# A hybrid RWKV/convolution trunk: a smaller descriptor memory, five raw weight buffers instead of three, three split pairs instead of two

## The chip, the cores and the metric

The kernel runs on one core of one Trainium2 chip. The metric is device time in microseconds of one execution. Before the change the median of three runs is 1274.27 us (1272.84 to 1274.8).

## The reference

One layer over 1024 tokens of width 1024, all in float32. A token mixer has an RWKV-7 recurrence on half of its channels (8 heads of 64) and a gated causal convolution of width 31 on the other half; both take their inputs from one projection and meet in one output projection. A gated feed-forward part with a causal convolution of width 3 follows. Each part stands between two RMS norms and has a residual connection.

```python
h = _rms_norm(x, norm_pre_mix[i])
mix, v_first = _hybrid_mixer(h, w_in_i, ...)     # p = h @ w_in; _wkv7; conv; ... @ w_out
x = x + _rms_norm(mix, norm_post_mix[i])
h = _rms_norm(x, norm_pre_ffn[i])
hid = _causal_dwconv(h @ ffn_up, ffn_conv_w, ffn_conv_b)      # 1024 -> 2 * 2816
gate, up = hid[..., :D_FF], hid[..., D_FF:]
x = x + _rms_norm((jax.nn.gelu(gate) * up) @ ffn_down, norm_post_ffn[i])
```

## The kernel before, in words

Every large product is made at float32 accuracy from three products of a faster kind. An operand is split in a high and a low part: ScalarE (ACT) casts the float32 tile to the rounded type, which gives the high part, and another engine subtracts that from the original, which gives the low part (`split`, L159 to L162). The matmuls are high times high, high times low and low times high; low times low is left out.

**Weights** come through `weight` (L164 to L184). It allocates a raw tile from the pool `wp` under the tag `wr`, which has three buffers, has SyncE (SP) issue the load (L170), allocates a pair `wh` and `wl` with two buffers each (L176), and splits: ACT makes `wh`, GpSimd (POOL) makes `wl`. In the last part, `ffn_down`, VectorE (DVE) makes `wl`. All of this is traced under a raised priority. A raw, `wh` or `wl` tile is 128 partitions by 512 float32, 2 KB of a partition. One pair feeds 12 matmuls of 512 columns. Some weights bypass the pair: those that `ffn_down` holds elsewhere (`held`), and those of the second half of the output projection (`home`). Weights of the input projection are used for both halves of the sequence; the first half stores the low part in HBM, and the second half loads it back (L178, L179, L183).

Three more places take a buffer of `wr` or of the pair: the two small LoRA matrices at the start (L236), and in `shared` the tile `t3` (L1023) and the pairs of the combined weights (L1028).

**The order of the work.** The sequence is worked on in two halves of 512 tokens, the recurrence in four quarters of 256 with four chunks of 64 each. `mixer` (L1245) writes down streams with priorities: the recurrence comes ahead of the norms, the convolution and the projections, so that the matmuls of the projections fill what the recurrence leaves free on TensorE. `w_out` (L794 on) multiplies a half by the output projection and stores it in `mixd`. `norm_ffn` (L839) loads `x` and `mixd` rows, makes the first norm of the FFN and its transposed, split activations `f`. The first 12 feed-forward column pairs of the first half (`ffn_pair`, L901) run beside the last quarter of the recurrence. `gates`, `ffn_pair` for the second half and `shared` (L1004) follow: the last ten column pairs, and the down projection, use a two-by-two scheme with seven block products instead of eight, for which weights and activations are added and subtracted. POOL makes these sums of weights (`four_sums` and `weight_sums`, L1054 to L1081).

Each engine runs its own instructions strictly in order, and SP issues nearly all DMAs in order. Where an instruction stands in its engine's order is not written by hand: `build` opens

```python
with tile.TileContext(nc, schedule_with_timeline_sim=True) as tc, ExitStack() as ctx:
```

which orders the traced instructions by priority along a simulated time line. The number of buffers enters this simulation, since an instruction that allocates a tile is held there until a buffer of its tag is free.

`kernel` (L1462) creates the program. A part of each SBUF partition is reserved for descriptors of DMAs that software generates, 16 KB unless said otherwise.

Of the kernel before, what the change touches and what calls it, by code (L numbers as in the profile page):

```python
# [13 lines left out]
F32 = mybir.dt.float32  # L14
F32R = mybir.dt.float32r
# [7 lines left out]
P = 128  # L23
# [3 lines left out]
HALF = 512  # L27
# [4 lines left out]
D_RWKV = 512  # L32
# [10 lines left out]
LN_EPS = 1e-5  # L43
GN_EPS = 64e-5

HELD = 5
DECAY = math.exp(-0.5)

# [50 lines left out]
class Trunk:  # L99
# [64 lines left out]
    def weight(self, src, shape, home=None, held=None, kept=None):  # L164


        with self.tc.high_priority():
            raw = (self.f2p.tile(shape, F32, tag="f2", name=self.nm("wr")) if held is self.hp else
                   self.wp.tile(shape, F32, tag="wr", bufs=3, name=self.nm("wr")))
            self.load = self.nc.sync.dma_start(raw, src)  # L170
            if held:
                hi, lo = self.pair("w", held)
            elif home:
                hi, lo = (home[0].tile(shape, F32R, tag=t, bufs=BUFS[t], name=self.nm("wm")) for t in home[1:])
            else:
                hi, lo = (self.wp.tile(shape, F32R, tag=t, bufs=2, name=self.nm(t)) for t in ("wh", "wl"))  # L176
            if kept and kept[0]:
                self.nc.scalar.copy(hi, raw)  # L178
                self.nc.sync.dma_start(lo.bitcast(F32), kept[1])  # L179
            else:  # L180
                self.low = self.split(hi, lo, raw, self.low_pool)[1]
        if kept and not kept[0]:
            self.nc.sync.dma_start(kept[1], lo.bitcast(F32))  # L183
        return hi, lo  # L184
# [31 lines left out]
    def setup_mixer(self, ctx):  # L216
        nc, tc, a = self.nc, self.tc, self.a
        pool = lambda name, bufs=1: ctx.enter_context(tc.tile_pool(name=name, bufs=bufs))
        cp = pool("mconst")
        self.mix = pool("mix")  # L220
        self.banks = {"pb": 2, "pc": 1, "pe": 2}
        self.xs = [self.psum.tile([P, 512], F32, name=f"xs{g}") for g in range(2)]
        self.wa = cp.tile([P, HALF], F32, name="wa")

        self.dw = cp.tile([P, 16 + 1024], F32, name="dw")
        nc.gpsimd.memset(self.dw[0:64, 528:1040], 0.0)
        self.Y = self.psum.tile([P, 512], F32, name="Y")


        self.lora = cp.tile([G_LORA, D_RWKV], F32, name="lora")
        nc.sync.dma_start(self.lora, a["lora"][:G_LORA, 2])
        self.lw = cp.tile([96, 2, D_RWKV], F32R, name="lw")
        for e in range(2):
            raw = self.wp.tile([P, D_RWKV], F32, tag="wr", bufs=3, name=self.nm("wr"))  # L236
            nc.sync.dma_start(raw, a["lora"][:, e])
            nc.scalar.copy(self.lw[:, e], raw[0:96])
            low = self.lw[64:96, e]
            nc.gpsimd.tensor_tensor(low, raw[64:96], low.bitcast(F32), ALU.subtract)  # L240
        self.lx = cp.tile([96, 2, QUARTER], F32R, name="lx")
        n = POFF["k_k"]
        self.omu = cp.tile([P, n], F32, name="omu")
        nc.vector.tensor_scalar(self.omu, self.params[:, :n], -1.0, 1.0, ALU.mult, ALU.add)

        self.hw0 = cp.tile([P, 8], F32, name="hw0")
        nc.vector.tensor_scalar(self.hw0, self.params[:, POFF["w0"]:POFF["w0"] + 8], 0.5, None, ALU.mult)
        self.ka = cp.tile([P, 8], F32, name="ka")
        ka = self.params[:, POFF["k_a"]:POFF["k_a"] + 4]
        nc.vector.tensor_scalar(self.ka[:, 0:4], ka, 0.5, None, ALU.mult)  # L250
        nc.vector.tensor_scalar(self.ka[:, 4:8], ka, -0.5, 1.0, ALU.mult, ALU.add)
        cw = self.params[:, POFF["cw"]:POFF["cw"] + 4 * CONV_W]
        nc.vector.tensor_scalar(cw, cw, 0.5, None, ALU.mult)
        self.carry = cp.tile([P, n], F32, name="carry")
        self.ccarry = cp.tile([P, 4, 32], F32, name="ccarry")[:, :, :CONV_W - 1]
# [748 lines left out]
    def shared(self, i, S, A22, act0, act1, raws):  # L1004

        nc = self.nc
        temp = lambda: self.f2p.tile([P, HALF], F32, tag="f2", name=self.nm("acc"))
        kview = lambda t: t.rearrange("p (k m) -> p k m", k=4)
        up = self.a["ffn_up"]

        def add(out, x, y):
            with self.tc.high_priority():
                nc.vector.tensor_tensor(out, x, y, ALU.add)

        if raws is None:
            T = lambda n: self.weight(kview(self.usums[n - 1]), [P, 4, P])
            b22 = lambda: self.weight(up[FT + i, 1], [P, 4, P])
        else:
            with self.tc.high_priority():
                b11, b12, b21, b22r = raws  # L1020
                for n in (1, 3, 0, 2):
                    self.load = nc.sync.dma_start(kview(raws[n]), up[n % 2 * FT + i, n // 2])
                t3 = self.wp.tile([P, HALF], F32, tag="wr", bufs=3, name=self.nm("t3"))  # L1023
                self.four_sums(b11, b12, b21, b22r, t3)

            def pair(raw):
                with self.tc.high_priority():
                    hi, lo = (self.wp.tile([P, HALF], F32R, tag=t, bufs=2, name=self.nm(t)) for t in ("wh", "wl"))  # L1028
                    self.low = self.split(hi, lo, raw, True)[1]
                return kview(hi), kview(lo)  # L1030

            T = lambda n: pair((b12, b11, t3, b21)[n - 1])
            b22 = lambda: pair(b22r)
        x, y, z = (self.bank() for _ in range(3))
        self.four(x, T(2), S[2], True, True)
        add(act1, act1, x)
        self.four(y, T(1), S[1], True, True)
        W = temp()
        add(W, act1, y)
        self.four(z, T(3), S[3], True, True)  # L1040
        add(x, W, z)
        self.four(y, b22(), S[4], False, True)
        add(y, act1, y)
        self.four(z, T(4), A22, False, True)
        add(z, act1, z)
        two = [temp() for _ in range(2)]
        self.taps(0, i, 1, y, two[0])
        nc.vector.tensor_tensor(act0, act0, two[0], ALU.mult)
        self.taps(1, i, 0, z, act1)
        nc.scalar.activation(z, act1, AF.Gelu_apprx_tanh)  # L1050
        self.taps(1, i, 1, x, two[1])
        nc.vector.tensor_tensor(act1, z, two[1], ALU.mult)
# [50 lines left out]
    def ffn_down(self, acts):  # L1103
# [58 lines left out]
        def hold(j, every=2):  # L1162

            if j % every == 1 and len(late) < HELD:
                late.append(self.weight(B(1, 1)(HT - HELD + len(late)), [P, 512], held=self.hp))

# [294 lines left out]

# [6 lines left out]
```

## Time and profile before

| what | value |
|---|---|
| median of 3 runs | 1274.27 us |
| the profiled execution | 1273.13 us |
| its span, first to last instruction | 1271.4 us |
| mean granted TensorE clock | 0.990 |
| raw weight loads, L170 | 256 KB each, 2.7 to 2.9 us from issue to landing |
| cast to `wh`, 128x512 | 0.62 us on ACT |
| `wl` on POOL, 128x512 | 1.31 us mean |
| `wl` on DVE, 128x512 | 0.69 us |
| DMA traffic | 185.70 MB, 146 GB/s on average |

PE is TensorE's matmuls and PEld its weight loads, which run beside them. Matmul ends are modelled, so a matmul of 512 columns is drawn with 0.39 us. In the view of waits a row says which engine and output tile waited, for what, the total in us, how many times, and the longest. L135 is the line of every matmul, L150 of every transpose, and L162 of every split, so the tile names tell which one is meant: `wh` and `wl` are weights, `h` and `f` activations, `pb`, `pe`, `xs`, `Y` and `pc` PSUM banks, `a` and `w` the split operands that `ffn_down` keeps elsewhere. SPq stands for a DMA issue on SP. A wait for several things is put down to the one that came last.

### The profile page before, as it was taken

Reading aid. Unit: us, or ns where it says so; the run is one execution under the profiler, and the core shown is the slowest. Engines: PE = TensorE matmul, PEld = TensorE weight load, DVE = VectorE, ACT = ScalarE, POOL = GpSimd, SP = SyncE. Lnnn points to the kernel's source line nnn. Section 1 sums busy time; section 2 is a strip of 40 time slices with the busy share of each in tenths; the row PEclk is TensorE's granted clock in tenths of the full one; section 3 lists DMA queues with packets and bytes.
Section 4 is the critical chain, followed back from the end, with each engine's and each line's share of the span. In section 5 each row is a group of like instructions: output and inputs, shape, how many; then the busy total and the mean of one; then the engine's idle time right before and its main releaser. Section 6 shows DMA issues by size and latency. Waiting matters only on the chain.

```text
span 1271.4 us, 23025 instructions
## 1 busy us (share of the span) xinstructions
PE 1220.3 (96%) x8460; PEld 990.1 (78%) x8460; DVE 891.2 (70%) x1540; ACT 731.1 (58%) x1518; POOL 495.4 (39%) x438
## 2 busy tenths in 40 slices
PE   6999989999999988999999999999999999999996
PEld 4767767787778877788789878778877888888885
DVE  5286998998679989997631165666356779479667
ACT  7563563655845766566744277776555556545451
POOL 4343320011113332344455369898588860000001
PEclk9999998999999999999999999999999999999999
DMA  7644342343343451232345398888522236336523
GB/s 242 173 133 141 117 134 75 94 134 124 110 135 86 122 183 66 85 84 84 101 132 166 112 336 299 292 305 268 173 65 73 79 127 222 99 98 194 173 76 133
DMA packets 105505, 185.70 MB, mean 146 GB/s; under 512 B 15184, under 2 KB 21712, under 8 KB 105392
## 3 DMA queue, kind: packets, MB, share of 16 engines
q1 hardware_dynamic: 105392, 184.23, 46.2%
q8 instruction: 67, 1.10, 0.4%
q14 instruction: 46, 0.38, 0.1%
HBM read 141.58 MB, written 42.60 MB: 145 GB/s over the span
## 4 chain that ended last, share of the span: by engine, by line
PE 55%; DVE 8%; DMA 3%; POOL 3%; issue 2%; ACT 2%; SPq 0%; POOLq 0%; DVEq 0%; ACTq 0%
PE pb L135 26%; PE pe L135 13%; PE xs L135 11%; PE Y L135 2%; DVE pc L416 2%; PE pc L135 2%; POOL wl L162 1%; DVE nrow L1116 1%; DVE x L1100 1%; POOL b L1056 1%; PE pc L150 1%; DMA pt<-mixd 1%; DMA m<-mixd 1%; PE pe L150 0%; DMA b<-ffn_down 0%
## 5 line engine op out<-in xcount | busy, mean ns | idle before, releaser
L162 POOL TENSOR_TENSOR wl<-wr,wh 128x512 fp32r<-128x512 f32 (+1 forms) x181 | 237.2, 1312 | 247.7 <-ACT wh L162 221.0
L162 ACT CAST wh<-wr 128x512 fp32r<-128x512 f32 (+1 forms) x220 | 135.5, 616 | 170.7 <-issue 43.9
L135 PE MATMUL pb<-h,wh 128*128 128x512 f32 (+3 forms) x720 | 229.5, 398 | 2.5 <-ACT wh L162 1.0
L135 PE MATMUL pb<-f,wh 128*128 128x512 f32 x696 | 219.0, 395 | 2.6 <-ACT wh L162 1.5
L416 DVE SCALAR_TENSOR_TENSOR pc<-c,params,pc 128x512 f32<-128x512 f32 x232 | 174.1, 750 | 8.8 <-ACT pc L413 4.8
L135 PEld LDWEIGHTS pb<-h,wh 128*128 128x128 f32 (+2 forms) x720 | 131.8, 188 | 34.9 <-ACT wh L162 2.6
L135 PEld LDWEIGHTS pb<-f,wh 128*128 128x128 f32 x696 | 130.0, 189 | 31.0 <-ACT wh L162 2.8
L135 PE MATMUL pb<-h,wl 128*128 128x512 f32 (+3 forms) x360 | 146.4, 407 | 2.3 <-POOL wl L162 2.1
L135 PE MATMUL pb<-f,wl 128*128 128x512 f32 x348 | 137.9, 397 | 1.5 <-POOL wl L162 1.5
L157 POOL TENSOR_TENSOR ss<-var,mhalf 128x1 f32<-128x1 f32 x16 | 11.0, 692 | 222.6 <-DVE ss L1097 198.2
L1056 POOL TENSOR_TENSOR b<-b,b 128x512 f32<-128x512 f32 x66 | 86.8, 1317 | 2.8 <-issue 0.9
L135 PE MATMUL pe<-f,wh 128*128 128x512 f32 x272 | 84.2, 391 | 0.1
L135 PEld LDWEIGHTS pb<-h,wl 128*128 128x128 f32 (+2 forms) x360 | 67.7, 188 | 20.7 <-POOL wl L162 4.5
L135 PEld LDWEIGHTS pb<-f,wl 128*128 128x128 f32 x348 | 65.7, 189 | 16.9 <-POOL wl L162 3.1
L135 PE MATMUL xs<-f,wh 128*128 128x512 f32 x200 | 62.0, 391 | 0.4 <-DVE act L953 0.4
L135 PEld LDWEIGHTS pe<-f,wh 128*128 128x128 f32 x272 | 50.9, 188 | 10.6 <-ACT wh L162 0.3
L899 DVE SCALAR_TENSOR_TENSOR pt<-pb,params,pt 128x511 f32<-128x511 f32 (+1 forms) x48 | 35.7, 743 | 30.0 <-ACT ecarry L892 29.5
L162 POOL TENSOR_TENSOR wl<-b,wh 128x512 fp32r<-128x512 f32 x36 | 47.0, 1307 | 21.7 <-ACT wh L162 19.8
L135 PE MATMUL pe<-f,wl 128*128 128x512 f32 x136 | 53.7, 395 | 0.7 <-POOL wl L162 0.7
L706 POOL TENSOR_TENSOR XG<-r,GE 64x256 f32<-64x256 f32 x30 | 20.4, 683 | 86.9 <-DVE r L725 82.0
L178 ACT CAST wh<-wr 128x512 fp32r<-128x512 f32 (+2 forms) x44 | 26.5, 604 | 43.1 <-PE pb L135 31.2
L162 ACT CAST wh<-b 128x512 fp32r<-128x512 f32 x36 | 22.2, 617 | 46.8 <-PE pb L135 18.9
(428 smaller groups left out, 2883.7 us busy)
## 6 DMA issues: line engine op xcount, KB each, us to landing
wr<-ffn_up SPq DMA_DIRECT2D x117, 256.0 KB, 2.8
wr<-w_in SPq DMA_DIRECT2D x80, 256.0 KB, 2.9
b<-ffn_down SPq DMA_DIRECT2D x44, 256.0 KB, 4.4
sums<-b SPq DMA_DIRECT2D x44, 256.0 KB, 4.0
wr<-sums SPq DMA_DIRECT2D x44, 256.0 KB, 2.7
lows<-wl SPq DMA_DIRECT2D x40, 256.0 KB, 3.3
wl<-lows SPq DMA_DIRECT2D x40, 256.0 KB, 2.7
b<-ffn_up SPq DMA_DIRECT2D x40, 256.0 KB, 2.7
```

The costliest lines, as they stand in the source:

```text
L135: return self.nc.tensor.matmul(out, lhsT, rhs, start=start, stop=stop, skip_group_check=skip)
L150: self.nc.tensor.transpose(out, in_, self.con("ident")[:n, :n])
L157: self.nc.gpsimd.tensor_tensor(out, v[:, :n], self.mhalf[:, :n], ALU.pow)
L162: return self.nc.scalar.copy(hi, src), eng.tensor_tensor(lo, src, hi.bitcast(F32), ALU.subtract)
L178: self.nc.scalar.copy(hi, raw)
L416: nc.vector.scalar_tensor_tensor(out, c[:, j:j + HALF], w(j), acc, ALU.mult, ALU.add)
L706: nc.gpsimd.tensor_tensor(x[64:128], R[64:128, gs], w.GE[64:128, c, gs].unsqueeze(2).broadcast_to([64, 4, CH]), ALU.mult)
L899: nc.vector.scalar_tensor_tensor(acc[:, o:], ps[:, :HALF - o], w(j), acc[:, o:], ALU.mult, ALU.add)
L1056: sub = lambda o, x, y, op=ALU.subtract: self.nc.gpsimd.tensor_tensor(o, x, y, op)
L1100: nc.vector.scalar_tensor_tensor(x, f[c], s[:, 1:2], x, ALU.mult, ALU.add)
L1116: nc.vector.tensor_tensor(out, a, b, op)
```

## The change

The raw tag gets five buffers instead of three, `wh` and `wl` get three each instead of two, at all places that name them, and the descriptor memory is set to 1024 bytes of a partition.

```diff
+RAW = 5
+PAIRS = 3
...
-                   self.wp.tile(shape, F32, tag="wr", bufs=3, name=self.nm("wr")))
+                   self.wp.tile(shape, F32, tag="wr", bufs=RAW, name=self.nm("wr")))
...
-                hi, lo = (self.wp.tile(shape, F32R, tag=t, bufs=2, name=self.nm(t)) for t in ("wh", "wl"))
+                hi, lo = (self.wp.tile(shape, F32R, tag=t, bufs=PAIRS, name=self.nm(t)) for t in ("wh", "wl"))
...
-            raw = self.wp.tile([P, D_RWKV], F32, tag="wr", bufs=3, name=self.nm("wr"))
+            raw = self.wp.tile([P, D_RWKV], F32, tag="wr", bufs=RAW, name=self.nm("wr"))
...
-                t3 = self.wp.tile([P, HALF], F32, tag="wr", bufs=3, name=self.nm("t3"))
+                t3 = self.wp.tile([P, HALF], F32, tag="wr", bufs=RAW, name=self.nm("t3"))
...
-                    hi, lo = (self.wp.tile([P, HALF], F32R, tag=t, bufs=2, name=self.nm(t)) for t in ("wh", "wl"))
+                    hi, lo = (self.wp.tile([P, HALF], F32R, tag=t, bufs=PAIRS, name=self.nm(t)) for t in ("wh", "wl"))
...
-    nc = bacc.Bacc("TRN2", target_bir_lowering=False, num_devices=1)
+    nc = bacc.Bacc("TRN2", target_bir_lowering=False, num_devices=1, dynamic_dma_scratch_size=1024)
```

## The prediction

> **What bounds the kernel now.** I read the span on the page first, then busy time by stage, then the waits of TensorE (PE, and PEld for its weight loads), and last the time lines around single waits. The stages, from the view by windows, say which engine sets the time:
>
> ```profile
> span 1271.4 us, 23025 instructions
> ```
> ```profile
> 32.00:456.00 424.00, 409.47 (x3808) 326.38 (x3808) 340.26 (x609) 250.39 (x502) 105.19 (x112) 0.98 0.41 121
> 456.00:497.00 41.00, 34.76 (x420) 26.31 (x416) 35.45 (x85) 28.28 (x74) 10.60 (x14) 0.96 0.43 147
> 497.00:1245.00 748.00, 739.74 (x4072) 607.89 (x4072) 476.86 (x744) 427.17 (x885) 360.09 (x283) 1.00 0.49 155
> ```
>
> A row of the second fence is one stretch: its length, then busy time of PE, PEld, DVE, ACT and POOL, the granted clock, the DMA share and GB/s. PE is the bound. It is idle 14.5 us in the mixer (32 to 456), 6.2 us in the handover to the FFN (456 to 497) and 8.3 us in the 748 us of FFN. No count of matmuls changes, so the change can win only idle time and stretched matmuls. Which of it belongs to weights, the waits of PE and PEld say; columns are total us, times, longest. First PE and PEld in the stretch 0 to 500, then both from 500 to 1050:
>
> ```profile
> PE pb L135 <- POOL wl L162: 3.0, 5, 1.1
> ...
> PE pb L135 <- ACT wh L162: 1.0, 1, 1.0
> PE pb L135 <- ACT wh L178: 0.9, 1, 0.9
> ```
> ```profile
> PEld pb L135 <- POOL wl L162: 5.5, 7, 1.5
> ...
> PEld pb L135 <- ACT wh L162: 2.9, 5, 1.2
> ```
> ```profile
> PE pb L135 <- ACT wh L162: 2.0, 3, 1.2
> PE pb L135 <- POOL wl L162: 1.9, 3, 0.9
> PE pe L135 <- ACT wh L162: 0.8, 1, 0.8
> PE pe L135 <- POOL wl L162: 0.7, 1, 0.7
> PE xs L135 <- POOL wl L162: 0.7, 2, 0.3
> ```
> ```profile
> PEld pe L135 <- POOL wl L162: 4.2, 11, 1.1
> PEld xs L135 <- POOL wl L162: 4.1, 9, 0.8
> PEld pb L135 <- POOL wl L162: 3.9, 6, 1.3
> PEld pb L135 <- ACT wh L162: 3.8, 4, 1.6
> ```
>
> So PE stands still for a split weight for 4.9 us in 7 waits before 500, and for 6.1 us in 10 waits after it: the largest removable item of the FFN's 8.3 us. PEld waits for the same tiles 8.4 us before and 16.0 us after. The true loss lies between, since a weight load that is late by less than its lead costs nothing.
>
> **Why a weight is late.** One wait in full, from the time line (start, length, what, idle time before it in brackets):
>
> ```profile
> 625.38 0.62 ACT L162 CAST wh<-wr 128x512 fp32r<-128x512 f32 x1
> ...
> 630.77 0.63 ACT L162 CAST wh<-wr 128x512 fp32r<-128x512 f32 x1
> ...
> 631.46 0.73 PE L135 MATMUL pb<-f,wh 128*128 128x512 f32 x2 [1.19 <-ACT wh L162]
> ```
> ```profile
> 1075.21 1.36 PE pe L135 x6
> ```
>
> ACT makes two casts of weights 5.4 us apart, because other work of ACT stands between them. The row in the second fence is PE at its pace, from the chain that ended last: 6 matmuls in 1.36 us, 0.227 us each. A weight pair feeds 12 matmuls, so 2.72 us. Two pairs last 5.4 us, one of them already in use: a burst of that length on ACT or POOL empties them. Three last 8.2 us.
>
> **The change part by part.** Descriptor memory: who uses DMA descriptors in memory is told by the queues.
>
> ```profile
> q1 hardware_dynamic: 105392, 184.23, 46.2%
> q8 instruction: 67, 1.10, 0.4%
> q14 instruction: 46, 0.38, 0.1%
> ```
>
> All of the program's data goes through one hardware queue, issued by SP, and the rest is instruction fetch; no queue of descriptors made by software exists. Cost of the smaller memory: 0, with nothing needed to hide it. It adds and removes no instruction. It frees 15 KB of a partition, and the tiles (2 KB each) take two raws and one pair, 8 KB.
>
> Third pair: the longest wait of PE is 1.2 us and of PEld 1.6 us, both below the 2.72 us that one more pair holds, so each single wait is covered if the engines get the time to fill the third pair beforehand. After 500 the loss is 6.1 us plus what the row of a matmul hides: the profile draws a matmul longer than its pace, 0.73 us for two against 0.45, so up to 0.28 us of each wait counts as busy. With 0.15 us each for 10 waits that is 7.6 us; PEld's 16.0 is the upper bound and 6.1 the lower. I take 9, nearer the PE rows, because most PEld waits have no PE wait behind them. I credit three quarters of it, 6.75 us, not all: in the worst part the filler itself is nearly full, as this row shows (POOL is the fifth engine).
>
> ```profile
> 768.00:800.00 32.00, 32.00 (x148) 26.30 (x147) 17.87 (x29) 23.94 (x52) 30.81 (x25) 1.00 0.87 297
> ```
>
> Before 500 the loss is 4.9 to 8.4 us, 6 to 7 by the same reckoning, and I credit 2.8: PE's time there is handed on only where PE decides. The first w_out matmuls wait for the recurrence, not for weights, and the handover is a chain of transfers, of which these are the first two:
>
> ```profile
> PE pe L150 <- DVE mixr L760: 2.2, 1, 2.2
> ```
> ```profile
> 456.50 4.28 DMA mixd<-t
> 461.22 3.37 DMA row<-x
> ```
>
> Five raws: they let SP issue loads earlier. What it waits for, and what ACT waits for:
>
> ```profile
> SPq L170 <- POOL wl L162: 52.7, 10, 18.3
> ```
> ```profile
> ACT wh L162 <- PE pb L135: 62.8, 39, 2.5
> ```
>
> The first is SP's wait for a raw buffer between 425 and 520, 5.3 us each on average; the second is ACT's wait to overwrite a pair that PE still reads, over the whole span. Both block work queued behind on the same engine. I book no gain of their own for them: a raw that comes earlier helps only through the pair it fills. No bytes are added, so the DMA share is unchanged in sum.
>
> What is added: nothing executes twice, but build() orders all engines by a simulated time line, so every order can move. No row prices that. The handover's idle time, 6.2 us, is the nearest row: it could double or go, so plus or minus 6.2, and I take 0 because it has no direction.
>
> One cost has one. When POOL splits a weight while DVE reads two operands from SBUF, DVE stretches:
>
> ```profile
> 70.50 0.68 DVE L493 TENSOR_TENSOR l<-row,pt 128x512 f32<-128x512 f32 x1
> ...
> 72.45 3.29 POOL L162 TENSOR_TENSOR wl<-wr,wh 128x512 fp32r<-128x512 f32 x2
> ...
> 74.64 1.66 DVE L510 TENSOR_TENSOR l<-pt,pt 128x512 f32<-128x512 f32 x1
> ```
>
> 0.98 us longer for the same shape. A pair that is filled ahead lets POOL run splits back to back, as in these two. I charge one such collision, 1.0 us, at places where DVE is on the path. [...]
>
> **The sum.** 6.75 + 2.8 - 1.0 = 8.5 us gained. The profiled execution took 1273.13 us, 1.7 over its span and 1.1 under the median of 1274.27; taken off the profiled execution that is 1264.6, on the scale of the median 1265.8, my forecast.
>
> **Rivals.** (a) More: ACT's 62.8 us of waiting go as well, and the evacuations queued behind come earlier. Half of the mixer's 14.5 us of idle PE would go on top, 7.2: 1258.6. For it: 39 such waits. Against it: in the mixer ACT is busy only 250 of 424 us, so what is queued behind those waits has room to catch up. (b) Rate, not depth: the filling engine is late in a row rather than in a burst, or the planner leaves the new buffers empty. POOL's 30.81 of 32 us speaks for it, PE's 17 waits, spread over both stretches with none above 1.2 us, against it. A quarter of 8.5 is left, 2.1: 1272.2, no change. [...] (d) Slower: the handover. Weight loads have high priority and SP issues in order. With more raws, further ffn_up loads can stand in SP's queue ahead of the row and mixd loads of the first FFN norm, each waiting for POOL to free a raw. Two such waits at 5.3 us lengthen the chain of transfers that begins above by 10.5; with only the gain of the FFN, 6.75, left, the result is 3.8 slower, 1278.1. It decides from the second wait on, and PE has no other work there. Against it: a larger supply also lets SP finish those loads before the handover begins.
>
> **How the numbers follow.** Forecast 0.50, (a) 0.12, (b) 0.17, (c) 0.05, (d) 0.16. About 0.2%, 2.5 us, is what a measurement of this kernel can tell from no change. Faster is the forecast with (a), 0.62; same is (b) with (c), 0.22; slower is (d), 0.16. The likeliest case's own range is 1260 to 1271, the gain between 3 and 14. The range is 1256 to 1278: it takes in (a), (b), (c) and most of (d), and the re-ordering's 6.2 us around the forecast; a cure of all 24 us of PEld waits lies outside, as does (d) with a third blocked load.
>
> **What would show it.** If right: PE's waits for wh and wl fall from 11.0 us to about 3 and PEld's from 24 to below 12; what is left lies between 730 and 1050; PE's busy time falls by the stretched matmuls, 2 to 4 us; ACT's waits on pb before wh shrink; SP's wait for a raw shrinks; the FFN stretch from the end of the handover to the last products is 5 to 8 us shorter. [...] The forecast is wrong if the wh and wl waits go and the span does not follow, or if the gain sits in the handover instead.

## The result: 10 us slower, the loss in the mixer

The changed kernel takes 1284.62 us, the median of four runs from 1282.96 to 1289.17, beside 1274.20 (1272.84 to 1274.80) for the kernel before: a ratio of 1.0089, with an interval of 1.0062 to 1.0116. The forecast was 1265.8 in a range of 1256 to 1278.

The profiled execution of the changed kernel is its longest, 1289.17 us at a mean granted clock of 0.968; the other three took 1282.96 to 1284.71 us at 0.976 to 0.978. So the two traces differ by 15.8 us of span where the medians differ by 10.4, and some 5 us of what the trace shows belong to this execution alone. Its code lies two lines lower, so L137, L152 and L164 are the matmuls, transposes and splits. From the page, the span and the granted clock in 40 slices:

```profile
span 1287.2 us, 23033 instructions
...
PEclk8999977999998988999999999999999999999998
```

The view by windows of the changed kernel, over the three stretches of the prediction (length, then busy us and instructions of PE, PEld, DVE, ACT and POOL, granted clock, DMA share, GB/s):

```profile
32.00:456.00 424.00, 403.22 (x3495) 318.43 (x3494) 317.61 (x579) 237.26 (x461) 97.70 (x105) 0.94 0.39 113
456.00:497.00 41.00, 34.69 (x452) 29.21 (x450) 32.10 (x54) 26.01 (x71) 13.23 (x12) 0.90 0.51 161
497.00:1245.00 748.00, 741.95 (x4281) 618.20 (x4282) 479.86 (x778) 435.18 (x906) 362.43 (x292) 0.99 0.49 158
```

Read the count behind PE first: in the 424 us of the mixer it has done 3495 matmuls, where it did 3808 before. The stretches no longer hold the same work, so their busy times cannot be subtracted. A fair cut is an event of the program: the first matmul of the FFN (`pb<-f,wh`) starts at 497.65 us before and at 528.16 after. Cut there, the same view, first of the kernel before:

```profile
32.00:497.00 465.00, 444.22 (x4222) 352.69 (x4220) 375.72 (x693) 278.67 (x576) 115.78 (x126) 0.98 0.41 124
497.00:1262.00 765.00, 756.52 (x4145) 621.44 (x4144) 492.02 (x779) 429.35 (x891) 365.28 (x289) 1.00 0.49 155
```

and of the changed kernel:

```profile
32.00:528.00 496.00, 464.70 (x4222) 369.57 (x4220) 377.69 (x704) 283.67 (x580) 115.98 (x126) 0.93 0.39 116
528.00:1278.00 750.00, 748.16 (x4144) 623.38 (x4144) 482.23 (x769) 427.94 (x889) 363.00 (x288) 1.00 0.49 157
```

Now the counts agree, and the change does two opposite things. The same 4222 matmuls up to the FFN take 496 us in place of 465; the same 4144 after it take 750 in place of 765. To a tenth, from the first FFN matmul to the last of the down projection, it is 750.0 in place of 764.1. The FFN won 14.1 us and the mixer lost 30.5.

The FFN's win is the one that was aimed at. Waits of PEld for a split weight over the whole span of the changed kernel (total us, times, longest):

```profile
PEld pb L137 <- ACT wh L164: 1.3, 1, 1.3
PEld xs L137 <- ACT wh L164: 0.8, 1, 0.8
PEld pe L137 <- ACT wh L180: 0.4, 1, 0.4
PEld pe L137 <- ACT wh L164: 0.4, 1, 0.4
PEld xs L137 <- POOL wl L164: 0.3, 1, 0.3
```

Single waits are left, and in the waits of PE itself, where 17 had stood, neither `wh` nor `wl` occurs any more. The largest waits of PE that are left, apart from the 9.5 us at the start (9.9 before):

```profile
PE xs L152 <- DVE r L727: 4.1, 3, 3.0
PE pe L152 <- ACT ck L558: 3.7, 2, 3.0
PE pb L152 <- DVE h L281: 3.0, 4, 1.4
PE pe L152 <- DVE mixr L748: 2.7, 2, 2.1
PE xs L137 <- ACT l L653: 2.6, 2, 1.9
```

The third is a wait for activations and stood at 2.5 us before. The other four are for results of the recurrence, and nothing filled PE while it waited for them.

**Where the loss begins.** The recurrence's first chunk, seen by its operations with each shape apart (count: duration in ns min/median/max, first and last start in us). The kernel before:

```profile
L135 PE MATMUL pe<-dw,l x128: 177/178/198, 134.5 to 136.5; 32*32 32x16 f32 x128
L150 PE MATMUL pe<-const,l x32: 187/188/202, 151.0 to 155.0; 32*32 32x32 f32 x32
...
L704 ACT COPY XG<-xs x32: 344/368/371, 166.2 to 596.8; 64x256 f32<-64x256 f32 x32
```

The changed kernel:

```profile
L137 PE MATMUL pe<-dw,l x128: 177/178/198, 142.6 to 144.6; 32*32 32x16 f32 x128
L152 PE MATMUL pe<-const,l x32: 188/188/199, 166.8 to 172.6; 32*32 32x32 f32 x32
...
L706 ACT COPY XG<-xs x32: 347/368/371, 178.9 to 636.3; 64x256 f32<-64x256 f32 x32
```

None of these operations is longer; each starts later. The small matmuls of the recurrence are 8.1 us late at the first row, the transposes 15.8, the first chunk's `XG` 12.7, and the last chunk's `XG` 39.5. What stands ahead of the transposes, the chain of waits of the changed kernel says, asked for 60 to 206 us (start, length, what):

```profile
146.72 1.62 PE pe L137 x2
148.34 5.26 PE pb L137 x18
153.60 2.01 PE pe L137 x129
155.61 5.45 PE pb L137 x24
161.06 0.24 PE pe L137 x2
161.30 5.22 PE pb L137 x23
```

The `pb` rows are projections. The row of 129 holds a second group of small matmuls of the recurrence, `pe<-l,dw`, which follows the one listed above; it starts at 141.80 us before and 153.53 after. The matmuls that read `h`, from the first group to the second and from the second to the transposes (PE busy and count, clock, DMA share, GB/s), before:

```profile
134.51:141.80 7.29, 4.67 (x19) 1.00 0.45 146
141.80:150.99 9.19, 7.22 (x31) 1.00 0.47 125
```

and after:

```profile
142.56:153.53 10.97, 6.25 (x19) 0.84 0.34 97
153.53:166.80 13.27, 11.35 (x49) 1.00 0.56 159
```

So the lateness has three parts here. The first group is 8.1 us late: the steps of DVE ahead of it are 4.5 us late at the first (`dw<-l`, 115.9 to 120.4), shortly after the chain has come over from PE's projections, and 7.0 at the last (`l<-dw`, 129.9 to 136.9). Up to the second group the delay grows to 11.7 us with the same 19 projection matmuls: PE waits 2.0 us for DVE's `kk`, and the granted clock is 0.84. Up to the transposes it grows to 15.8, because 49 projection matmuls stand ahead of them in PE's order where 31 had stood.

Projections are the work that is meant to fill gaps. How much of it PE does in two longer stretches, the same view tells, before:

```profile
96.00:134.00 38.00, 30.67 (x119) 1.00 0.44 130
176.00:204.00 28.00, 10.31 (x38) 0.88 0.24 76
```

and after:

```profile
96.00:134.00 38.00, 32.94 (x132) 1.00 0.51 149
176.00:204.00 28.00, 1.65 (x3) 0.53 0.06 20
```

Thirteen more are done in the first stretch (29 more counted from 32 us, 376 in place of 347), and then, while the recurrence's small serial steps run and the second half's activations are not ready, 3 are left in place of 38. The granted clock there is 0.53. The skipped time is not made up: the last projection matmul ends at 403.7 us in place of 385.8, and `w_out` of the first half begins at 413.1 in place of 389.9. The delay of 12.7 us at the first chunk is thus 23.2 at `w_out` and 30.5 at the first FFN matmul; which wait adds which part on the way was not followed.

### The profile page after: what moved, and what is told of

Its sections match the earlier page's. It is cut to its first block, busy times and chain, and to the rows that moved or that the text cites. A ratio compares the mean times of both kernels' runs of the same rounds, so it can differ in the third digit from the quotient of the medians.

```text
span 1287.2 us, 23033 instructions
## 1 busy us (share of the span) xinstructions
PE 1231.5 (96%) x8460; PEld 1008.4 (78%) x8460; DVE 884.4 (69%) x1540; ACT 734.9 (57%) x1520; POOL 494.1 (38%) x438
## 4 chain that ended last, share of the span: by engine, by line
PE 83%; DVE 10%; ACT 3%; DMA 2%; issue 1%; SPq 0%; POOL 0%; DVEq 0%; POOLq 0%; ACTq 0%
PE pb L137 42%; PE pe L137 18%; PE xs L137 17%; PE Y L137 2%; DVE pc L418 2%; PE pc L137 2%; PE pe L152 1%; PE pc L152 1%; DVE sub L593 1%; DMA mixd<-t 0%; DVE h L281 0%; PE xs L152 0%; DMA l<-x 0%; DVE dw L595 0%; DVE dw L584 0%
## 5 line engine op out<-in xcount | busy, mean ns | idle before, releaser
L164 POOL TENSOR_TENSOR wl<-wr,wh 128x512 fp32r<-128x512 f32 (+1 forms) x181 | 235.7, 1305 | 233.7 <-ACT wh L164 211.7
L137 PE MATMUL pb<-h,wh 128*128 128x512 f32 (+3 forms) x720 | 232.8, 400 | 2.4 <-DVE row L352 1.7
L137 PE MATMUL pb<-f,wh 128*128 128x512 f32 x696 | 219.3, 394 | 1.6 <-DVE pt L901 1.0
L164 ACT CAST wh<-wr 128x512 fp32r<-128x512 f32 (+1 forms) x220 | 135.2, 616 | 135.4 <-PE pb L137 48.4
L137 PEld LDWEIGHTS pb<-h,wh 128*128 128x128 f32 (+2 forms) x720 | 132.8, 190 | 34.0 <-DVE row L352 1.9
L137 PEld LDWEIGHTS pb<-f,wh 128*128 128x128 f32 x696 | 129.6, 188 | 28.9 <-ACT wh L164 1.3
L137 PE MATMUL pb<-h,wl 128*128 128x512 f32 (+3 forms) x360 | 143.4, 398 | 0.0
L137 PE MATMUL pb<-f,wl 128*128 128x512 f32 x348 | 136.9, 393 | 0.0
L159 POOL TENSOR_TENSOR ss<-var,mhalf 128x1 f32<-128x1 f32 x16 | 11.4, 718 | 227.5 <-DVE var L158 222.9
L137 PE MATMUL pe<-f,wh 128*128 128x512 f32 x272 | 83.9, 390 | 0.0
L137 PEld LDWEIGHTS pb<-h,wl 128*128 128x128 f32 (+2 forms) x360 | 68.2, 189 | 15.9 <-issue 0.5
L137 PEld LDWEIGHTS pb<-f,wl 128*128 128x128 f32 x348 | 65.5, 188 | 13.5
L137 PE MATMUL xs<-f,wh 128*128 128x512 f32 x200 | 62.2, 391 | 0.4 <-DVE act L955 0.4
L137 PEld LDWEIGHTS pe<-f,wh 128*128 128x128 f32 x272 | 51.0, 188 | 10.5
L164 POOL TENSOR_TENSOR wl<-b,wh 128x512 fp32r<-128x512 f32 x36 | 50.2, 1397 | 12.2 <-ACT wh L164 12.0
L137 PE MATMUL pe<-f,wl 128*128 128x512 f32 x136 | 53.2, 391 | 0.0
L164 ACT CAST w<-wr 128x512 fp32r<-128x512 f32 x38 | 23.6, 622 | 45.7 <-PE pe L137 23.4
L164 ACT CAST a<-act 128x512 fp32r<-128x512 f32 x50 | 29.8, 619 | 32.8 <-PE Y L137 18.4
```

The lines of the kernel that those rows point to most:

```text
L137: return self.nc.tensor.matmul(out, lhsT, rhs, start=start, stop=stop, skip_group_check=skip)
L159: self.nc.gpsimd.tensor_tensor(out, v[:, :n], self.mhalf[:, :n], ALU.pow)
L164: return self.nc.scalar.copy(hi, src), eng.tensor_tensor(lo, src, hi.bitcast(F32), ALU.subtract)
```

## The experiments

Three theories were open once both traces lay side by side. R: the planner's new order does it. B: the deeper buffers do it on the chip, by earlier loads and splits that collide with something. M: the descriptor memory matters. And for the FFN: is its gain the buffers' own, or the order's? All twelve kernels make the whole computation. Where an order is pinned, a function `keep_order` chains the traced instructions of one or more engines in an order recorded from another build, by dependencies that fix the order of issue and add no semaphore; whatever is not pinned is planned anew.

**The memory alone.** In the kernel before, only the last hunk of the diff:

```diff
-    nc = bacc.Bacc("TRN2", target_bir_lowering=False, num_devices=1)
+    nc = bacc.Bacc("TRN2", target_bir_lowering=False, num_devices=1, dynamic_dma_scratch_size=1024)
```

> Only the descriptor memory is cut to 1 KB; three raws and two pairs as before; every engine has the same instructions in the same order as before. Theory R (the planner's new order makes the loss) and theory B (the deeper buffers themselves make it, by running ahead into other work) both expect the time of before, 1272 to 1276 us. A rival M, that the smaller memory itself costs something, expects 1280 us or more.

Measured: 1273.20 us in one run, beside 1273.86 for the kernel before. M is out.

**The buffers in the old order.** The changed kernel, with every engine pinned to the order of the kernel before, from start to end:

```diff
         Trunk(ctx, tc, a).run()
+        keep_order(nc, tc)     # all engines, the whole program, order of the kernel before
```

> The whole change (1 KB, five raws, three pairs), but every engine's instructions are pinned to the order that they had before the change, instruction for instruction, by edges that set the order of issue and nothing else. Theory R expects the mixer back (first FFN matmul near 498 us instead of 528, half-clock time near 28 us instead of 84) and a part of the weight waits gone: 1264 to 1271 us. Theory B expects the loss to stay: 1280 us or more.

Measured: 1268.69 us (1268.09 to 1271.24) beside 1273.86, ratio 0.9962 (0.9946 to 0.9978). The first FFN matmul is at 497.5 us, where it was. So B is out for the loss: five raws and three pairs as such cost nothing. But they also bring little: 5.2 us by the medians. In the profiled execution, at 1270.88 us 2.2 above its median, the FFN stretch, by windows,

```profile
497.00:1259.00 762.00, 752.62 (x4143) 622.68 (x4144) 488.13 (x776) 425.41 (x891) 365.58 (x289) 1.00 0.47 155
```

is 762 us, only some 2 shorter, and PE still waits for weights, 11.1 us in 17 waits, of which the two largest rows are

```profile
PE pb L137 <- POOL wl L164: 3.5, 7, 1.1
PE xs L137 <- POOL wl L164: 2.3, 3, 1.3
```

while the row of ACT's waits to overwrite a pair, 62.8 us before, is nearly empty:

```profile
ACT wh L164 <- PE pb L137: 6.3, 3, 2.3
```

This is the most instructive run. ACT hardly waits for a free pair, and PE waits for weights as often as ever. The time line at the wait that the prediction showed in full has the same two casts of weights,

```profile
624.97 0.62 ACT L164 CAST wh<-wr 128x512 fp32r<-128x512 f32 x1
...
630.36 0.63 ACT L164 CAST wh<-wr 128x512 fp32r<-128x512 f32 x1
```

again 5.4 us apart, with other work of ACT between them. In ACT's fixed order a cast stands behind the same burst, whatever buffers are free; a buffer does not fill itself.

**One part each.**

```diff
-PAIRS = 3
+PAIRS = 2     # raws alone; the other kernel has RAW = 3 and PAIRS = 3
```

> Five raws, two pairs, 1 KB; the order is planned anew. Theory R expects some new order, so a shift of either sign that no count of buffers predicts, 1265 to 1290 us, with the loss or gain in the mixer (before 500 us) and PE's waits for wh and wl hardly changed, 8 to 11 us. Theory B in the form that SP's early loads do harm expects 1280 us or more.

> Three raws, three pairs, 1 KB; the order is planned anew. Theory R expects PE's waits for wh and wl below 3 us, an FFN stretch 8 us shorter or more, and a mixer that is shifted by its new order: 1262 to 1288 us. Theory B in the form that splits made ahead do harm expects 1280 us or more and the mixer's loss of 30 us as with the whole change.

Measured: raws alone 1280.96 us, ratio 1.0057 (1.0037 to 1.0076); pairs alone 1278.84, ratio 1.0038 (1.0027 to 1.0049). They lose in different places. With raws alone the FFN starts at 499.4 and its stretch is 768.5 us, 4.4 longer than before, where the expectation had put the shift in the mixer. With pairs alone it starts at 515.1 and takes 752.3: both the loss of the mixer and the win of the FFN come with the third pair. Matmuls that read `h`, with pairs alone:

```profile
96.00:134.00 38.00, 33.10 (x132) 1.00 0.50 147
176.00:204.00 28.00, 4.53 (x11) 0.70 0.06 19
```

The same signature as the changed kernel's, without a single raw more.

**The old order in the mixer alone.** The changed kernel with instructions pinned up to the first FFN matmul: of all engines, of TensorE, of VectorE, of ScalarE.

```diff
         Trunk(ctx, tc, a).run()
+        keep_order(nc, tc)     # up to the first f matmul: all engines | PE | DVE | ACT
```

> The whole change, with every engine pinned to the old order only up to the first matmul that reads f, the end of the mixer; from there the order is planned anew. Theory R: the mixer ends as before, first f matmul near 498 us, and the stretch from there to the last matmul of the down projection keeps the 750 us that the whole change has (764 before): 1256 to 1263 us. Rival S: the short FFN of the changed kernel came only from a recurrence that its late mixer had left over in another state; then the stretch is 760 us or more and the time 1267 to 1274 us.

> As e5, but in the mixer only TensorE keeps the old order; ACT, DVE, GpSimd and SP are planned anew. If the loss is made by TensorE's order (projection matmuls, ready earlier, go ahead of the recurrence and are missing later), the mixer ends near 498 us and the time is 1256 to 1264 us. If it is made by the order on ACT or DVE (casts of weights ahead of recurrence and convolution work), the mixer ends at 508 us or later and the time is 1268 us or more.

> As e5, but in the mixer only DVE keeps the old order. If DVE's order (convolution steps against recurrence and norm) makes the loss, the mixer ends near 498 us; if TensorE's or ACT's does, at 508 us or later.

> As e5, but in the mixer only ACT keeps the old order. If ACT's casts of weights ahead of the recurrence's own ACT work make the loss, the mixer ends near 498 us; if TensorE's or DVE's order does, at 508 us or later.

| order kept in the mixer | median us | first FFN matmul | FFN stretch |
|---|---|---|---|
| none (the change) | 1284.62 | 528.2 | 750.0 |
| all engines | 1265.84, ratio 0.9926 (0.9908 to 0.9944) | 499.6 | 756.1 |
| TensorE | 1264.70, ratio 0.9919 (0.9894 to 0.9944) | 500.8 | 752.7 |
| VectorE (one run) | 1290.66 | 524.6 | 755.1 |
| ScalarE (one run) | 1275.48 | 507.9 | 756.8 |

Holding TensorE's order is enough to bring the mixer back. Both times lie a little above what was expected, since the FFN keeps 8.0 and 11.4 of its 14.1 us. The windows of the kernel with TensorE held, cut at its own first FFN matmul, and its matmuls that read `h`:

```profile
32.00:501.00 469.00, 446.01 (x4227) 355.56 (x4226) 378.51 (x701) 281.09 (x580) 117.15 (x126) 0.97 0.41 123
501.00:1253.00 752.00, 746.89 (x4143) 622.45 (x4143) 486.05 (x771) 429.78 (x889) 360.82 (x288) 1.00 0.49 157
```
```profile
96.00:134.00 38.00, 30.79 (x117) 1.00 0.46 129
176.00:204.00 28.00, 11.18 (x42) 0.88 0.21 62
```

117 and 42, close to the 119 and 38 before the change, and 469 us for the work that took 496. This does not mean that TensorE's order works by itself, since the planner arranges the other engines around it. Compared by their tile names in the traces, up to the first FFN matmul, 99% of DVE's instructions and over 99% of ACT's stand in the order of the kernel before, though they were planned anew; in the changed kernel it is 52% and 67%. What the run shows is that holding TensorE brings the old plan back.

VectorE's order does not help, though it is exactly the old one: the first chunk's `XG` is at 171.6 us there and 128 `h` matmuls stand ahead. ScalarE's does in part, but its planner, held by it, also puts TensorE back (113 matmuls, `XG` at 165.3), so that run does not speak for ScalarE by itself either.

**The new order with the old buffers.** The reverse: the kernel before, three raws, two pairs and 16 KB, with TensorE pinned up to the first FFN matmul to the order of the changed kernel.

```diff
         Trunk(ctx, tc, a).run()
+        keep_order(nc, tc)     # PE, up to the first f matmul, order of the changed kernel
```

> The reverse of e6: three raws, two pairs and the large descriptor memory as before the change, but TensorE is pinned in the mixer to the order that the changed kernel has; the rest is planned anew. If TensorE's order makes the loss by itself, the mixer ends at 520 us or later (498 before, 528 changed) although no buffer was added, and the time, without the FFN's gain, is 1288 us or more. If the order is bad only together with the deeper buffers, the mixer ends at 510 us or earlier and the time is below 1283 us.

Measured: 1307.28 us (1304.19 to 1308.68), ratio 1.0250 (1.0232 to 1.0268). The first FFN matmul is at 530.7 and the FFN stretch 764.6, the old one. The windows:

```profile
32.00:531.00 499.00, 459.36 (x4222) 359.89 (x4221) 375.10 (x705) 283.65 (x580) 116.49 (x126) 0.96 0.39 115
531.00:1295.00 764.00, 755.45 (x4144) 619.77 (x4142) 483.67 (x765) 430.85 (x890) 363.94 (x289) 1.00 0.49 156
```

The whole loss of the mixer comes back with no buffer changed. Together with the run that kept TensorE's old order, this shows the planned order to be the cause, and not the depth of the buffers: putting it in makes the loss, taking it out removes it. Here too the other engines follow TensorE, as 97% of DVE's and of ACT's instructions stand in the changed kernel's order, so a share of TensorE's own is not told apart.

It also bounds the clock. The part of these stretches that the granted clock left out is 0.02 of 465 us before, 0.07 of 496 in the changed kernel and 0.04 of 499 here, or some 9, 35 and 20 us. By this estimate lost clock can cost no more than that, so it makes at most 11 of the 34 us that this mixer loses. In the changed kernel the bound is 25 of 31, and what the clock really cost there stays open.

**A repair by hand, and the dose.** If two pairs keep the mixer's order and three serve the FFN, a third pair that only the FFN may use should win both without pinning.

```diff
+    def weight_pair(self, shape):
+        x = "x" * next(self.third)
+        return tuple(self.wp.tile(shape, F32R, tag=t + x, bufs=1 if x else PAIRS, name=self.nm(t)) for t in ("wh", "wl"))
...
+        self.third = cycle((0, 0, 1))     # from the first norm of the FFN on; (0,) until then, and PAIRS = 2
```

> Five raws and 1 KB, but the third pair has a tag of its own that is used, every third time, only by weights traced from the FFN's first norm on; the mixer's projections have two pairs. Nothing is pinned. If the third pair lets the projections run ahead in the mixer, that is undone: mixer end near 500 us as with five raws alone, FFN stretch 750 to 757 us, time 1260 to 1269 us. If any new plan loses by chance, the mixer ends at 508 us or later and the time is 1272 us or more.

Measured: 1273.58 us (1270.79 to 1274.91) beside 1275.62, ratio 0.9982 (0.9972 to 0.9993): a miss. The mixer is near the old one, with the first FFN matmul at 503.7, but the FFN stretch of 758.8 wins 5.3 us and not 12, and PE has a new wait there:

```profile
PE pb L138 <- DVE pt L906: 6.1, 2, 5.5
```

The plan of the FFN came out another way again. The last two runs vary the counts, four raws with three pairs and five raws with four pairs:

```diff
-RAW = 5
+RAW = 4     # the other kernel: RAW = 5, PAIRS = 4
```

> Four raws, three pairs, planned anew. If three pairs make the mixer's loss through projections that run ahead, the mixer ends at 512 us or later, as with three raws (515) and five (528), and the FFN stretch is 750 to 757 us: 1275 to 1290 us. If the loss is a chance of one plan, the mixer may end near 498 us.

> Five raws, four pairs, planned anew. If more pairs mean more projections ahead, the mixer ends at 525 us or later and the time is 1280 us or more, since the FFN has no waits for weights left to lose. If the loss is a chance of one plan, the mixer may end earlier than 515 us.

Measured, one run each: 1279.76 and 1282.29 us, first FFN matmul at 517.5 and 520.4, FFN stretches 751.4 and 750.7. For four pairs the mixer had been expected to end at 525 us or later. A fourth pair does not lose more than the third, so the loss is no smooth function of the count; but each plan with three or four pairs that leaves TensorE free and pins nothing has 132 or 133 `h` matmuls in 96 to 134 us, and each with two up to there has 118 or 119. These counts are a mark of the plan; that moving just these matmuls makes the loss was not tested.

## Why the prediction was wrong, point by point

**The bound and the cure were right.** PE bounds the kernel, late weights cost it time, and with a third pair the waits of PE for `wh` and `wl` and those of PEld go: forecast about 3 us and below 12, found single waits of 1.3 us or less.

**The FFN term was mis-sized.** 6.75 us was booked, three quarters of 9; 14.1 was found. Idle time of PE in the equal work fell from 8.5 us (765 less 756.52) to 1.8, and PE's busy time by 8.4, where 2 to 4 had been allowed for stretched matmuls. The result lies near the 16.0 us of PEld's waits that the prediction had as its upper bound, but that is in part luck: most of it came only with the new order, as the next point says. The bound itself was added up from some of the rows. The rest of that view has PEld waits for `wh` of tile `pe` (0.4 us before 500 and 1.5 after) and for the `wh` of L178 (1.7), so the full sums are 10.5 and 17.5 us where 8.4 and 16.0 were read.

**Its reason was half right.** The step "a third pair covers a burst of 8.2 us" takes it that the engines fill the pair when it is free. The run with the old order has the free pair, and 11.1 us of waits all the same. About 2 us of the FFN's win are the buffers' own in the profiled execution, 5.2 us of the whole time by the medians; the rest needs casts and splits to move forward in their engines' orders. PE's waits for weights go in the changed kernel and stay, 17 of them, where only the buffers were added.

**The step that failed is the re-ordering**, "plus or minus 6.2, and I take 0 because it has no direction". It measured +30.5 us in the mixer, five times the bound, and some -12 of the FFN's -14.1 come only with it as well. It also had a direction: every free plan with a third pair in the mixer ends it late, at 515 to 528 us. The handover's idle time was the wrong nearest row: by these traces, what a new order can cost is not the idle time that stands in one stage, but how far a serial chain can be pushed back and what filler is missing when it then runs alone. PE was idle only 14.5 us in the mixer, with 38 projection matmuls in the 28 us where the change left 3; that filler was the reserve at stake. So the 2.8 us booked for weights before 500 were not won either: with TensorE's mixer order kept, PE has one wait for a weight left, of 2.2 us in the whole span, and the mixer still ends 3.1 us later than before.

**The slower rival named another mechanism.** It put the loss into the handover, by `ffn_up` loads ahead of `mixd` loads on SP. From the end of the first half's `w_out` to the first FFN matmul it is 42.4 us before (455.2 to 497.6) and 44.4 after (483.8 to 528.2): 2.0 us of 30.5. The result, 1284.62, lies 6.5 above that rival's 1278.1.

**The rest.** The descriptor memory at 0: right, by the run of it alone. "No gain of their own" for the raws: too kind, alone they lose 0.57%, by another plan whose detail was not followed. Rival (a), ACT's waits: the changed kernel keeps them (63.2 us in 40), and the run that cut them to 6.3 us has its first FFN matmul at 497.5, so no shorter mixer. The 1.0 us for a stretched DVE operation: in the trace before, L510 takes 1.66 us at its longest beside a median of 0.69, but DVE's busy time over both stretches is 867.7 us before and 859.9 after, so more of such stretching does not show in the sum. Nor do the runs show anything for (c). Rival (b) described the run with the old order, where the new buffers stay of little use, and not the change. The prediction had named its own refutation, "the wh and wl waits go and the span does not follow"; it came true.

**The forecast's size was reachable.** With TensorE's mixer order kept, the change measures 1264.70 us, 0.81% faster (interval 0.56 to 1.06%), the best version of the study. That it lies so near the forecast is partly luck, as its FFN is 11.4 us shorter and its mixer 3.1 longer.

**Left open.** Which engine's order, and which of the moved matmuls, make the loss within the new plan; how much of it is lost clock; why raws alone lengthen the FFN; why the late third pair leaves the mixer 6 us late and gets a 5.5 us wait; why four pairs lose less in the mixer than three. That the planner moves projections forward because a freed pair makes them look ready sooner fits all plans with two, three and four pairs, but its simulated time line was not looked into.

## What to carry to other kernels

Where a planner sets the order, a buffer count is also an input to the order of every engine, and what it does there can outweigh the waits it was raised for: test it once with every engine pinned to the old order, and once in the new order with the old count. Compare stretches of equal work, cut at an event of the program, because stretches of equal time would have hidden here that the FFN won and the mixer lost. Filler that is placed early in an engine's order can cost twice, once for the serial chain behind it (49 projection matmuls ahead of the transposes in place of 31) and once when it is missing later (3 in 28 us in place of 38); here the traces show both, and the experiments the order as a whole.

## What the runs showed of the hardware

With 3 projection matmuls left in 28 us, the granted clock of TensorE falls to 0.53, though the small matmuls of the recurrence go on: 225 matmuls in all run there. The windows of the changed kernel around the drop, of all instructions, the first from the end of the last projection matmul ahead of it:

```profile
175.13:177.90 2.77, 1.59 (x40) 1.12 (x40) 1.95 (x4) 2.66 (x6) 0.82 (x2) 1.00 0.52 180
177.90:208.70 30.80, 26.47 (x271) 20.62 (x271) 28.24 (x46) 17.36 (x39) 1.46 (x2) 0.50 0.01 2
```

In the 2.8 us ahead of the drop PE is drawn busy for 1.59 us. Then it has a clock of 0.50 for 30.8 us, and is drawn busy for 26.47 of them. Over 134 to 204 us the drawn busy time hardly differs, while the clock goes from 0.95 before to 0.79 after:

```profile
134.00:204.00 70.00, 65.30 (x773) 51.30 (x774) 67.29 (x98) 41.85 (x82) 19.79 (x25) 0.95 0.38 114
```
```profile
134.00:204.00 70.00, 62.28 (x693) 47.28 (x693) 64.82 (x100) 39.24 (x75) 15.29 (x19) 0.79 0.31 91
```

So a drawn busy share near 0.9 (62.28 of 70.00 us) did not keep the clock up. It is no exact measure of PE's work, since ends of matmuls are modelled. What lets the clock fall is not settled by these runs: 40 matmuls run in the 2.8 us ahead of the drop.
